# Layer 0 attention: q's rms norm moved from the projected q to the exponential's factor

## The chip, the cores and the metric

The kernel runs on one core of one Trainium2 chip. Five engines of that core work side by side and wait for each other by semaphores: TensorE (PE; its weight loads are listed apart, as PEld), VectorE (DVE), ScalarE (ACT), GpSimd (POOL) and SyncE (SP), which starts most transfers. The metric is the time of one execution on the device in microseconds (us). Three executions of the kernel before took 2746.94, 2752.83 and 2753.98 us; their median is 2752.83 us.

## The reference

The program is a trunk of four layers on 512 latent tokens and 256 context tokens of width 1024, each layer with another mixer (attention, neighbourhood attention, convolution, Fourier) and an MLP. The change is in the mixer of layer 0 alone. Cut to what matters there:

```python
def rms_norm(x, g):
    y = xf * lax.rsqrt(jnp.mean(xf * xf, axis=-1, keepdims=True) + EPS)
    return (y * g.astype(jnp.float32)).astype(x.dtype)

def gqa_attend(q, k, v):
    s = jnp.einsum('bqkgd,bnkd->bkgqn', q, k, preferred_element_type=jnp.float32)
    p = jax.nn.softmax(s, axis=-1).astype(v.dtype)
    return jnp.einsum('bkgqn,bnkd->bqkgd', p, v)

def gqa_mixer(hl, hc, ang, w_qkv, q_g, k_g, w_o, ctx_out):
    scale = HEAD_DIM ** -0.5
    ql = apply_rope(rms_norm(ql.reshape(B, S, AT_HEADS, HEAD_DIM), q_g), ang) * scale
    kl = apply_rope(rms_norm(kl.reshape(B, S, AT_KV_HEADS, HEAD_DIM), k_g), ang)
    ...
    qc = rms_norm((hc @ w_qkv[:, :AT_WIDTH]).reshape(B, C, AT_HEADS, HEAD_DIM), q_g) * scale
    oc = gqa_attend(qc.reshape(B, C, AT_KV_HEADS, AT_GROUP, HEAD_DIM), kc, vc)
```

There are 16 query heads of 64 columns. The norm divides each query's 64 values by one number, which is a factor common to all scores of that query and head.

## The kernel before

Matrix products are made in two parts each (a value rounded to fp32r and its remainder), so that one product costs three matmuls (`mm3`, lines 119 to 127: L124, L125, L127).

**Projection stage (`l0a`).** Keys and values are already in PSUM when it begins. Then come the queries in 12 units: four groups of columns `g` by three pairs of token tiles `tp` (`tp` 0 and 1 are the latent tokens, `tp` 2 the context). A unit is 48 matmuls into one PSUM bank (`ps_mm`, four banks in turn, so that the matmuls of a unit can start when the bank of the unit four before it has been read for the last time). Units are collected in `wait`; after every second one `finish` handles both. `qk_norm` squares a unit on ScalarE (L490) and sums by head on VectorE (L491), for both units, and calls `rstd` once: a square root on ScalarE (L133) and five small VectorE instructions (L135 to L139). `qk_unit` then multiplies the PSUM bank by the result on VectorE (L499), which is the last read of the bank, and rotates: for `tp` below 2 two GpSimd products (L511), a VectorE product (L512) and a GpSimd sum (L513); for `tp` 2 only a VectorE product with the gain (L515). ScalarE rounds the unit (L104 of `split`, into `pk`), VectorE takes the remainder (L105), TensorE transposes (L527), ScalarE copies out (L529), and a DMA stores it to HBM (L530). Beside this VectorE works off products for the modulation vectors (L223).

**Attention stage (`l0b`).** It takes over the four banks of `ps_mm` as two buffers `ps_s` of two banks each. The work is 8 pairs of heads; a pair is 12 fronts (128 queries of one head): 8 fronts with 768 keys and 4 of the context with 256 keys. A front is: score matmuls (L612), the negated maximum on VectorE (L614, `small_m`), the exponential on ScalarE with that maximum as bias and with the row sum as a second output (L616), TensorE transposes of the result `p` (L621), and for each group of up to three transposes a rounding copy on ScalarE (L104) and a remainder on VectorE (L105), both into `pt`. The products with v follow one head later (L635), and a closing per head pair (L555, L557, L559, L561, L567, L568, L573).

**What sets the order.** The program is not run in the order in which it is written: a scheduler reorders the instructions of each engine when the kernel is built, from its own estimate of durations; only instructions marked to keep their order (the loads among them) stay. Every engine then works its list strictly in order, so an instruction that waits holds up all behind it on that engine. The last two query units are finished inside the attention's loop (`late`, at `i == LATE`).

## Time and profile before

| | |
|---|---|
| median of three executions | 2752.83 us |
| the profiled execution's own time | 2748.76 us |
| its span | 2747.0 us |
[...]
| busy share TensorE, VectorE, ScalarE, GpSimd | 96%, 65%, 42%, 15% |
| projection of q, taken as 79 to 183 us | 104.0 us |
| attention, taken as 183 to 384.4 us | 201.4 us |

A row of the timeline gives start, length, engine, line, operation and tiles (output<-inputs), and in brackets the idle time before it with what ended it. TensorE's matmuls overlap in the pipeline: a row's length (0.28 us for 256 columns) is more than the distance from one start to the next (0.12 us). On VectorE and ScalarE too the next instruction may start a little (0.08 to 0.1 us) before the end of the one before. The profiled execution is one of the kernel's, and 4.07 us below the median of the three.

### The profile page before, as it was taken

How to read it: one execution, taken by the hardware profiler on the slowest of the kernel's cores; microseconds unless marked ns; L12 is line 12 of the kernel's file. 1: busy time of each engine (PE TensorE's matmuls, PEld its weight loads, DVE VectorE, ACT ScalarE, POOL GpSimd, SP SyncE). 2: the span in 40 equal slices, each digit the busy share in tenths (PEclk: the TensorE clock that was granted, in tenths of full speed). 3: DMA queues.
4: the chain of work that ended last, by engine and by line, in shares of the span. 5: the costliest groups of instructions: out<-in, count | busy, mean ns of one | idle time of the engine just before them, and what ended most of it. 6: DMA issues, size and time to landing. Idle time of an engine off the chain costs nothing.

```text
span 2747.0 us, 39895 instructions
## 1 busy us (share of the span) xinstructions
PE 2638.0 (96%) x15472; PEld 2316.5 (84%) x15472; DVE 1776.1 (65%) x2827; ACT 1154.8 (42%) x2052; POOL 405.4 (15%) x359
## 2 busy tenths in 40 slices
PE   7989899999999999998999999998999998999998
PEld 5878778888888888988988889888888887988888
DVE  7988879766453372268766657998666657644445
ACT  3458864212121342268523335656322245533323
POOL 2321212000000030034200004543000012200002
PEclk8999999999999999999999999999999999999999
DMA  7431234445442256488466644213466633333334
GB/s 269 133 123 36 77 120 147 139 145 153 137 140 85 77 168 209 138 201 190 161 206 207 190 147 139 77 47 107 133 212 200 206 124 107 123 115 94 98 100 123
DMA packets 124844, 384.85 MB, mean 140 GB/s; under 512 B 17264, under 2 KB 37872, under 8 KB 123632
## 3 DMA queue, kind: packets, MB, share of 16 engines
q1 hardware_dynamic: 121392, 379.17, 44.2%
q10 hardware_dynamic: 3264, 3.15, 0.3%
q8 instruction: 122, 2.00, 0.3%
q14 instruction: 66, 0.54, 0.1%
HBM read 354.98 MB, written 27.26 MB: 139 GB/s over the span
## 4 chain that ended last, share of the span: by engine, by line
PE 49%; DVE 4%; DMA 2%; ACT 1%; issue 0%; POOL 0%; DVEq 0%; SPq 0%; ACTq 0%; POOLq 0%
PE ps_mm L124 15%; PE ps_mm L125 15%; PE ps_mm L127 15%; DVE ps_st L1162 1%; DMA k<-k 1%; DMA q<-q 1%; PE ps_cv L124 1%; PE ps_cv L125 1%; PE ps_cv L127 1%; DVE h L182 0%; PE ps_s L881 0%; PE ps_pt L890 0%; PE ps_cv L995 0%; PE ps_cv L998 0%; PE ps_cv L999 0%
## 5 line engine op out<-in xcount | busy, mean ns | idle before, releaser
L104 ACT CAST wh<-raw 128x1024 fp32r<-128x1024 f32 (+1 forms) x397 | 419.6, 1060 | 1030.6 <-PE ps_mm L125 606.5
L105 DVE TENSOR_TENSOR wl<-raw,wh 128x1024 fp32r<-128x1024 f32 (+1 forms) x368 | 463.7, 1262 | 372.6 <-ACT wh L104 369.5
L194 POOL TENSOR_TENSOR S<-S,tmp_q 128x256 f32<-128x256 f32 (+1 forms) x104 | 144.8, 1392 | 1684.8 <-ACT tmp_q L193 1680.7
L124 PE MATMUL ps_mm<-u,wh 128*128 128x512 f32 (+1 forms) x1088 | 374.9, 346 | 0.0
L125 PE MATMUL ps_mm<-u,wh 128*128 128x512 f32 (+1 forms) x1088 | 373.8, 345 | 0.0
L127 PE MATMUL ps_mm<-u,wl 128*128 128x512 f32 (+1 forms) x1088 | 373.6, 346 | 0.0
L125 PE MATMUL ps_mm<-hm,wh 128*128 128x512 f32 (+1 forms) x912 | 331.2, 365 | 0.0
L127 PE MATMUL ps_mm<-hm,wl 128*128 128x512 f32 (+1 forms) x912 | 331.0, 365 | 0.0
L124 PE MATMUL ps_mm<-hm,wh 128*128 128x512 f32 (+1 forms) x912 | 328.2, 366 | 1.1 <-ACT hm L181 1.1
L223 DVE CUSTOM_DVE_ANT_0 prod<-araw,sb 128x1024 bf16<-128x1024 f32 x224 | 276.4, 1234 | 6.5 <-DMA araw<-in_ada 5.3
L206 DVE SCALAR_TENSOR_TENSOR x<-ps_mm,mod,x 128x256 f32<-128x256 f32 (+1 forms) x192 | 115.1, 605 | 246.8 <-PE ps_mm L127 241.1
L125 PEld LDWEIGHTS ps_mm<-u,wh 128*128 128x128 f32 x1088 | 206.1, 189 | 25.0
L127 PEld LDWEIGHTS ps_mm<-u,wl 128*128 128x128 f32 x1088 | 205.9, 189 | 25.2
L124 PEld LDWEIGHTS ps_mm<-u,wh 128*128 128x128 f32 x1088 | 205.7, 189 | 25.3 <-DVE x L206 0.4
L127 PEld LDWEIGHTS ps_mm<-hm,wl 128*128 128x128 f32 x912 | 172.6, 189 | 27.6 <-DVE wl L105 0.4
L125 PEld LDWEIGHTS ps_mm<-hm,wh 128*128 128x128 f32 x912 | 172.7, 190 | 27.2
L124 PEld LDWEIGHTS ps_mm<-hm,wh 128*128 128x128 f32 x912 | 170.8, 190 | 28.7 <-ACT hm L181 1.5
L104 ACT CAST u<-tmp_r 128x512 fp32r<-128x512 f32 (+2 forms) x143 | 89.0, 624 | 171.1 <-DVE tmp_r L738 170.9
L124 PE MATMUL ps_big<-hm,wh 128*128 128x512 f32 x464 | 157.4, 339 | 0.8 <-ACT wh L104 0.8
L105 DVE TENSOR_TENSOR u<-tmp_r,u 128x512 fp32r<-128x512 f32 (+2 forms) x143 | 99.1, 695 | 86.6 <-ACT u L104 86.2
L125 PE MATMUL ps_big<-hm,wh 128*128 128x512 f32 x464 | 145.9, 337 | 0.0
L124 PE MATMUL ps_mm<-wh,h 128*128 128x256 f32 x448 | 129.9, 291 | 7.3 <-DVE tmp_r L499 2.9
(311 smaller groups left out, 5781.6 us busy)
## 6 DMA issues: line engine op xcount, KB each, us to landing
raw<-in_w SPq DMA_DIRECT2D x288, 512.0 KB, 3.9
araw<-in_ada SPq DMA_DIRECT2D x176, 512.0 KB, 3.7
raw<-in_wo SPq DMA_DIRECT2D x32, 512.0 KB, 4.3
raw<-in_wpw SPq DMA_DIRECT2D x24, 512.0 KB, 3.5
raw<-in_wqk SPq DMA_DIRECT2D x16, 512.0 KB, 4.1
q<-q SPq DMA_DIRECT2D x32, 256.0 KB, 9.1
raw<-in_wft SPq DMA_DIRECT2D x16, 512.0 KB, 3.8
k<-k SPq DMA_DIRECT2D x32, 224.0 KB, 9.4
```

Source lines behind the costliest of these rows:

```text
L104: self.nc.scalar.copy(out=H, in_=src)
L105: (low or self.nc.vector).tensor_tensor(out=L, in0=src, in1=H.bitcast(F), op=ALU.subtract)
L124: mm(o, lhs[0], rh, start=(k == 0), stop=False)
L125: mm(o, lhs[0], rl, start=False, stop=False)
L127: mm(o, lhs[1], rh, start=False, stop=last)
L194: (add or nc.gpsimd).tensor_tensor(out=S[:, :w], in0=S[:, :w], in1=q, op=ALU.add)
L206: self.nc.vector.scalar_tensor_tensor(out=xm, in0=self.like(ps), scalar=gate[:, m:m + 1], in1=xm, op0=ALU.mult, op1=ALU.add)
L223: ins = self.nc.vector.tensor_tensor_reduce(out=junk, in0=t, in1=self.sb[:, v], op0=ALU.mult, op1=ALU.add, scale=1.0, scalar=0.0, accum_ou ...
L1162: keep(nc.vector.scalar_tensor_tensor(out=y if last else a, in0=ut, scalar=wt, in1=a, op0=ALU.mult, op1=ALU.add))
```

## The change

The sum of squares and `rstd` remain, but q's result no longer multiplies q. It is kept by query and head in a new tile `rsq` (four groups of 24 numbers), and the attention uses it twice per front: a new VectorE instruction (L630) multiplies the negated maximum by it, and the exponential (now L632) takes it as its factor. In `qk_unit` the multiplication of q (12 of the 15 at L499; it stays for k, now L505) is gone. For `tp` below 2 ScalarE copies the bank to SBUF (L509), GpSimd's two products (L523) read that copy, and VectorE's own product (now L525) reads the bank itself; for `tp` 2 the product with the gain (now L528) reads the bank. `rstd` is called once per group of three units (four times, on 24 columns) where it was called once per two (six times, on 16). Units are finished one by one and not in twos; only the last two wait for `late`.

```diff
         ve.tensor_tensor(out=v, in0=v, in1=y, op=ALU.mult)
         ve.tensor_tensor(out=v, in0=v, in1=y, op=ALU.mult)
-        last = ve.scalar_tensor_tensor(out=y, in0=v, scalar=1.5, in1=y, op0=ALU.add, op1=ALU.mult)
+        out = y if out is None else out
+        last = ve.scalar_tensor_tensor(out=out, in0=v, scalar=1.5, in1=y, op0=ALU.add, op1=ALU.mult)
         if pin:
             self.tc.keep_in_program_order(last)
-        return y
+        return out
 
     def bcast(self, cols, nb):
...
@@ -446,15 +448,23 @@
         for tp in range(3):
             pv = self.kv_ps[1][tp].rearrange("p (t h d) -> p t h d", t=2, h=4)
             self.split(pv, *(self.vp[:, 2 * tp:2 * tp + 2, :, s] for s in range(2)))
-        rs = self.qk_norm(self.kv_ps[0])
+        ss = self.small(24, "h")
         for tp in range(3):
-            self.qk_unit(self.kv_ps[0][tp], rs[tp], tp, 1, 0, wk, tab, qkg)
+            self.squares(self.kv_ps[0][tp], ss, tp)
+        rs = self.rstd(ss, HD, "h")
+        for tp in range(3):
+            self.qk_unit(self.kv_ps[0][tp], rs[:, 8 * tp:8 * tp + 8], tp, 1, 0, wk, tab, qkg)
             self.pump(1)
-        wait = []
+        wait, sums = [], {}
 
         def finish():
-            for a, r in zip(wait, self.qk_norm([a[0] for a in wait])):
-                self.qk_unit(a[0], r, a[1], 0, a[2], wk, tab, qkg)
+            for ps, tp, g in wait:
+                if tp == 0:
+                    sums[g] = self.small(24, "h")
+                self.squares(ps, sums[g], tp)
+                self.qk_unit(ps, None, tp, 0, g, wk, tab, qkg)
+                if tp == 2:
+                    self.rstd(sums[g], HD, "h", out=self.rsq[:, g])
                 self.pump(1)
             wait.clear()
 
@@ -468,7 +478,7 @@
                     for k in range(KC):
                         self.mm3([o], (h[k][:, 0, t0:t0 + P], h[k][:, 1, t0:t0 + P]), [(W[0][:, k], W[1][:, k])], k, k == KC - 1)
                 wait.append((ps, tp, g))
-                if len(wait) == 2 and (g, tp) != (3, 2):
+                if g < 3 or tp == 0:
                     finish()
         self.drain()
 
...
@@ -480,24 +490,26 @@
         self.close("h0", "ada", "wide")
         self.open_weights(3)
 
-    def qk_norm(self, pss):
+    def squares(self, ps, ss, tp):
+
+        sq = self.tmp("q")
+        self.nc.scalar.activation(sq, ps, AF.Square)
+        self.nc.vector.tensor_reduce(out=ss[:, 8 * tp:8 * tp + 8], in_=sq.rearrange("p (n d) -> p n d", d=HD), axis=AX.X, op=ALU.add)
+
+    def qk_unit(self, ps, rs, tp, a, g, wk, tab, qkg):
+
 
         nc = self.nc
-        n = len(pss)
-        ss = self.small(8 * n, "h")
-        for i, ps in enumerate(pss):
-            sq = self.tmp("q")
-            nc.scalar.activation(sq, ps, AF.Square)
-            nc.vector.tensor_reduce(out=ss[:, 8 * i:8 * i + 8], in_=sq.rearrange("p (n d) -> p n d", d=HD), axis=AX.X, op=ALU.add)
-        rs = self.rstd(ss, HD, "h")
-        return [rs[:, 8 * i:8 * i + 8] for i in range(n)]
-
-    def qk_unit(self, ps, rs, tp, a, g, wk, tab, qkg):
-
-        nc = self.nc
-        qn = self.tmp("r")
-        nc.vector.tensor_tensor(out=qn.rearrange("p (n d) -> p n d", d=HD), in0=ps.rearrange("p (n d) -> p n d", d=HD),
-                                in1=rs.unsqueeze(2).to_broadcast([P, 8, HD]), op=ALU.mult)
+        if rs is not None:
+            qn = self.tmp("r")
+            nc.vector.tensor_tensor(out=qn.rearrange("p (n d) -> p n d", d=HD), in0=ps.rearrange("p (n d) -> p n d", d=HD),
+                                    in1=rs.unsqueeze(2).to_broadcast([P, 8, HD]), op=ALU.mult)
+        elif tp < 2:
+            qn = self.tmp("r")
+            nc.scalar.copy(out=qn[:, :512], in_=ps)
+        else:
+            qn = ps
+        qn = qn[:, :512]
         q4 = qn.rearrange("p (t h d) -> p t h d", t=2, h=4)
         o = self.newS()
         o4 = o.rearrange("p (t h d) -> p t h d", t=2, h=4)
@@ -509,7 +521,8 @@
                 q5 = q4[:, t].rearrange("p h (s e) -> p h s e", s=2)
                 s5 = tab[:, a, 1, c].rearrange("p (s e) -> p s e", s=2).unsqueeze(1).to_broadcast([P, 4, 2, HD // 2])
                 nc.gpsimd.tensor_tensor(out=b4[:, t].rearrange("p h (s e) -> p h s e", s=2), in0=q5[:, :, ::-1, :], in1=s5, op=ALU.mult)
-            nc.vector.tensor_tensor(out=o4, in0=q4, in1=tab[:, a, 0, 2 * tp:2 * tp + 2].unsqueeze(2).to_broadcast([P, 2, 4, HD]), op=ALU.mult)
+            c4 = q4 if rs is not None else ps.rearrange("p (t h d) -> p t h d", t=2, h=4)
+            nc.vector.tensor_tensor(out=o4, in0=c4, in1=tab[:, a, 0, 2 * tp:2 * tp + 2].unsqueeze(2).to_broadcast([P, 2, 4, HD]), op=ALU.mult)
             nc.gpsimd.tensor_tensor(out=o, in0=o, in1=b, op=ALU.add)
         else:
             nc.vector.tensor_tensor(out=o.rearrange("p (n d) -> p n d", d=HD), in0=qn.rearrange("p (n d) -> p n d", d=HD),
@@ -612,8 +625,11 @@
                     nc.tensor.matmul(ps[:, c0:c1], q[:, hh, t0:t0 + P], self.kd[:, pair // 2, s, c0:c1], start=(s == 0), stop=(s == 1))
             mx = self.small(1, "m")
             nc.vector.tensor_reduce(out=mx, in_=ps[:, kc:TALL], axis=AX.X, op=ALU.max, negate=True)
+            n = part * 8 + u * 4 + pair % 2 * 2 + hh
+            rs = self.rsq[:, pair // 2, n:n + 1]
+            nc.vector.tensor_tensor(out=mx, in0=mx, in1=rs, op=ALU.mult)
             p = wk.tile([P, TALL], F, tag="p", name="p", bufs=3)
-            nc.scalar.activation(p[:, kc:], ps[:, kc:TALL], AF.Exp, bias=mx, accum_out=sums[:, u, hh:hh + 1])
+            nc.scalar.activation(p[:, kc:], ps[:, kc:TALL], AF.Exp, bias=mx, scale=rs, accum_out=sums[:, u, hh:hh + 1])
             for c in range(k0, 6, 3):
                 n = min(3, 6 - c)
                 pp = self.ps("st")

```

The build order shows three places. The first is VectorE at the end of the projection stage, from the sums of squares of the last unit to the first maximum of the attention. Before:

```order
L491 TENSOR_REDUCE small_h<-tmp_q 128x8
L135 TENSOR_SCALAR small_hv<-small_h 128x16
L136 RECIPROCAL small_hy<-small_hr 128x16
L137 TENSOR_TENSOR small_hv<-small_hv,small_hy 128x16
L138 TENSOR_TENSOR small_hv<-small_hv,small_hy 128x16
L139 SCALAR_TENSOR_TENSOR small_hy<-small_hv,small_hy 128x16
L499 TENSOR_TENSOR tmp_r<-ps_mm,small_hy 128x512 x2
L512 TENSOR_TENSOR S<-tmp_r,tab 128x512
L515 TENSOR_TENSOR S<-tmp_r,qkg 128x512
L614 TENSOR_REDUCE small_m<-ps_s 128x1 x2
```

In the changed kernel, from the last but one unit's product on (the squares are now L497, the maximum L627):

```order
L525 TENSOR_TENSOR S<-ps_mm,tab 128x512
L105 TENSOR_TENSOR pk<-S,pk 128x8x64
L497 TENSOR_REDUCE small_h<-tmp_q 128x8
L528 TENSOR_TENSOR S<-ps_mm,qkg 128x512
L135 TENSOR_SCALAR small_hv<-small_h 128x24
L136 RECIPROCAL small_hy<-small_hr 128x24
L137 TENSOR_TENSOR small_hv<-small_hv,small_hy 128x24
L138 TENSOR_TENSOR small_hv<-small_hv,small_hy 128x24
L105 TENSOR_TENSOR pk<-S,pk 128x8x64
L140 SCALAR_TENSOR_TENSOR rsq<-small_hv,small_hy 128x24
L627 TENSOR_REDUCE small_m<-ps_s 128x1
L630 TENSOR_TENSOR small_m<-small_m,rsq 128x1
```

Before, the last reads of the PSUM banks (L499) stand behind the five small instructions; now the last reads (L525 and L528) stand ahead of them, and the small instructions have only the first maximum behind them.

The second is VectorE inside the attention, from maximum 27 to maximum 29 of 96 (the third pair of heads). Before:

```order
L614 TENSOR_REDUCE small_m<-ps_s 128x1
L105 TENSOR_TENSOR pt_2696<-ps_st,pt_2695 128x384 x2
L568 TENSOR_TENSOR tmp_t<-ps_pv,tmp_t 64x256
L614 TENSOR_REDUCE small_m<-ps_s 128x1
L105 TENSOR_TENSOR pt_2696<-ps_st,pt_2695 128x384 x2
L614 TENSOR_REDUCE small_m<-ps_s 128x1
L568 TENSOR_TENSOR tmp_t<-ps_pv,tmp_t 64x256
```

In the changed kernel:

```order
L627 TENSOR_REDUCE small_m<-ps_s 128x1
L105 TENSOR_TENSOR pt_2693<-ps_st,pt_2692 128x384
L630 TENSOR_TENSOR small_m<-small_m,rsq 128x1
L581 TENSOR_TENSOR tmp_t<-ps_pv,tmp_t 64x256
L105 TENSOR_TENSOR pt_2693<-ps_st,pt_2692 128x384 x2
L627 TENSOR_REDUCE small_m<-ps_s 128x1
L630 TENSOR_TENSOR small_m<-small_m,rsq 128x1
L105 TENSOR_TENSOR pt_2760<-ps_st,pt_2759 128x384
L627 TENSOR_REDUCE small_m<-ps_s 128x1
L568 RECIPROCAL rs<-sums 128x4
L630 TENSOR_TENSOR small_m<-small_m,rsq 128x1
```

The new product L630 stands behind its maximum L627, in most fronts not straight behind it but with one or more others between them (a remainder L105 here, the reciprocal of a head pair there).

The third is ScalarE at the same place, exponentials 27 to 29. The number in `pt` names the head: 2695 is that of exponentials 25 and 26; 2760 before and 2759 after that of exponentials 27 and 28. Before:

```order
L616 ACTIVATE p,sums<-ps_s,small_m 128x768
L104 CAST pt_2695<-ps_st 128x384 x2
L567 COPY tmp_t<-ps_pv 64x256
L561 COPY tmp_r<-ps_st 128x256
L616 ACTIVATE p,sums<-ps_s,small_m 128x768
L104 CAST pt_2760<-ps_st 128x384 x2
L616 ACTIVATE p,sums<-ps_s,small_m 128x768
```

In the changed kernel:

```order
L632 ACTIVATE p,sums<-ps_s,small_m,rsq 128x768
L574 COPY tmp_r<-ps_st 128x256
L104 CAST pt_2759<-ps_st 128x384
L104 CAST o_1_1921<-tmp_t 128x256
L632 ACTIVATE p,sums<-ps_s,small_m,rsq 128x768
L104 CAST pt_2759<-ps_st 128x384 x2
L632 ACTIVATE p,sums<-ps_s,small_m,rsq 128x768
```

Before, the copies between exponential 27 and 28 were those of exponential 26's front, and the copies of front 27 came behind exponential 28. Now a copy of front 27 itself (the first `pt_2759`) stands between exponentials 27 and 28, and one of front 28 between 28 and 29: most long exponentials now have a copy of the front just ahead of them on ScalarE's list before them.

## Rows read from the trace of the kernel before

**Rows 1.** busy us by engine: start:end length, PE, PEld, DVE, ACT, POOL, clock, DMA

```profile
79.00:183.00 104.00, 91.56 (x712) 89.13 (x712) 97.12 (x161) 44.69 (x74) 37.74 (x30) 0.94 0.45 148
183.00:384.40 201.40, 179.86 (x1274) 159.17 (x1274) 174.03 (x354) 174.00 (x454) 39.18 (x48) 0.97 0.13 45
236.36:260.04 23.68, 21.84 (x159) 19.34 (x159) 21.41 (x45) 21.05 (x57) 4.43 (x6) 1.00 0.10 35
```

**Rows 2.** TensorE's waits in 78:183: who waited, for whom, us in total, times, longest

```profile
PE ps_s L612 <- DVE tmp_r L499: 4.3, 1, 4.3
...
PE ps_mm L124 <- DVE tmp_r L499: 2.9, 2, 1.8
...
PE ps_st L527 <- DVE pk L105: 1.0, 1, 1.0
```

**Rows 3.** timeline, TensorE: start us, us, engine line op [idle before <-releaser]

```profile
145.96 0.39 PE L124 MATMUL ps_mm<-wh,h 128*128 128x256 f32 x1 [1.75 <-DVE tmp_r L499]
```

**Rows 4.** the windows around that stop, columns as in rows 1

```profile
147.40:150.90 3.50, 3.50 (x19) 3.50 (x18) 3.26 (x8) 1.18 (x3) 1.59 (x2) 0.51 1.00 386
150.90:168.00 17.10, 17.00 (x146) 16.80 (x145) 17.02 (x28) 6.72 (x12) 8.11 (x6) 1.00 0.53 182
```

**Rows 5.** instructions grouped by line in 78:183: busy us, mean ns of one

```profile
L104 ACT CAST pk<-S 128x512 fp32r<-128x512 f32 x10 | 6.1, 620 | 11.6 <-POOL S L513 10.2 <-DVE S L515 1.4
...
L499 DVE TENSOR_TENSOR tmp_r<-ps_mm,small_hy 128x512 f32<-128x512 f32 x14 | 9.0, 685 | 0.3
```

**Rows 6.** timeline, VectorE, end of the projection stage

```profile
171.97 0.68 DVE L105 TENSOR_TENSOR pk<-S,pk 128x512 fp32r<-128x512 f32 x1
...
176.66 0.69 DVE L491 TENSOR_REDUCE small_h<-tmp_q 128x8 f32<-128x512 f32 x1 [1.50 <-ACT tmp_q L490]
...
180.03 1.29 DVE L499 TENSOR_TENSOR tmp_r<-ps_mm,small_hy 128x512 f32<-128x512 f32 x2
```

**Rows 7.** timeline, ScalarE, the same stretch

```profile
176.03 0.60 ACT L490 ACTIVATE tmp_q<-ps_mm 128x512 f32<-128x512 f32 x1 [0.62 <-PE ps_mm L127]
...
178.71 0.31 ACT L133 ACTIVATE small_hr<-small_h,eps 128x16 f32<-128x16 f32 x1
179.03 1.28 ACT L616 ACT_TABLE_LOAD   x1
184.13 0.90 ACT L616 ACTIVATE p<-ps_s,small_m 128x768 f32<-128x768 f32 x1 [3.82 <-DVE small_m L614]
```

**Rows 8.** instructions grouped by line in five attention periods: busy us, mean ns

```profile
L105 DVE TENSOR_TENSOR pt<-ps_st,pt 128x384 fp32r<-128x384 f32 x80 | 42.7, 549 | 3.3 <-ACT pt L104 2.4
...
L614 DVE TENSOR_REDUCE small_m<-ps_s 128x1 f32<-128x768 f32 x41 | 38.9, 949 | 0.3
...
L104 ACT CAST pt<-ps_st 128x384 fp32r<-128x384 f32 x80 | 37.4, 489 | 6.0 <-PE ps_st L621 5.7
...
L616 ACT ACTIVATE p<-ps_s,small_m 128x768 f32<-128x768 f32 x40 | 36.5, 913 | 0.1
...
L616 ACT ACTIVATE p<-ps_s,small_m 128x256 f32<-128x256 f32 x20 | 9.8, 491 | 0.4
```

**Rows 9.** timeline, ScalarE, one exponential in the attention

```profile
235.31 0.91 ACT L616 ACTIVATE p<-ps_s,small_m 128x768 f32<-128x768 f32 x1
```

**Rows 10.** timeline, TensorE, the transposes behind it, and one pair later

```profile
236.36 0.55 PE L621 MATMUL ps_st<-ident,p 128*128 128x128 f32 x3 [0.40 <-ACT p L616]
...
260.04 0.55 PE L621 MATMUL ps_st<-ident,p 128*128 128x128 f32 x3 [0.39 <-ACT p L616]
```

**Rows 11.** timeline, VectorE: small instructions, unchained and chained

```profile
122.04 0.16 DVE L135 TENSOR_SCALAR small_hv<-small_h 128x16 f32<-128x16 f32 x1
122.12 0.24 DVE L136 RECIPROCAL small_hy<-small_hr 128x16 f32<-128x16 f32 x1
...
149.93 0.18 DVE L137 TENSOR_TENSOR small_hv<-small_hv,small_hy 128x16 f32<-128x16 f32 x1
150.14 0.17 DVE L138 TENSOR_TENSOR small_hv<-small_hv,small_hy 128x16 f32<-128x16 f32 x1
```

More of the change, by code (lines that the diff above doesn't have):

```diff
@@ L127, in mm3, with rstd @@
             mm(o, lhs[1], rh, start=False, stop=last)
-    def rstd(self, ss, n, role="n", pin=False):
+    def rstd(self, ss, n, role="n", pin=False, out=None):
         w = ss.shape[-1]
@@ L433, in l0a @@
         self.vp = kv.tile([P, 6, 4, 2, HD], R, name="vp")
+        self.rsq = kv.tile([P, 4, 24], F, name="rsq")
         self.qd = self.dram.tile([8, P, 2, TALL], F, name="qd")
```

## The prediction

> **What bounds the kernel now.** I read the table of the page first: TensorE is busy 96% of the span, so outside the two stages of the change there is little to win, and the change's effect has to be looked for in the busy times by stretch [rows 1]. In the projection stage (79 to 183 us) VectorE is busy 97.12 of 104.00 us and TensorE 91.56; ScalarE has more than half of its time free. So TensorE sets the pace there, with VectorE close behind it: TensorE's list of waits says on whom it stops [rows 2]. It stopped 4.3 us once, at the handover to the attention, and 2.9 us in two stops, both for L499, the multiplication of q that the change takes out, and 1.0 us for a remainder (`pk`). The reader is to see that it is not L499's own length that costs: 0.685 us [rows 5]. The instruction is late because the sums of two units, a square root and five small instructions have to come first.
>
> In the attention everything is balanced: in one head pair's period VectorE is busy 21.41 of 23.68 us, ScalarE 21.05, TensorE 21.84 [rows 1]. TensorE restarts at the same point of the pattern at 236.36 and 260.04, each time after a stop for an exponential [rows 10], which is where I take the period of 23.68 from. No engine is full, so the period is set by the three waiting for each other; anything that is added to the path from the scores to the exponential can lengthen it.
>
> **Part 1, the two stops of the projection stage.** A bank is now free once ScalarE has squared and copied it and VectorE has made one product of it, within its own unit, and it is wanted again only four units later. The two stops go: 2.9 us [rows 2]. [...]
>
> **Part 2, the handover.** Before: the last unit is squared at 176.03 [rows 7], its sum starts at 176.66 [rows 6], the square root only gets its turn at 178.71 behind copies [rows 7], L499 reads the banks at 180.03 [rows 6], and the first exponential starts at 184.13 [rows 7]. After, from the same 176.03: sum to 177.35 (176.66 + 0.69); the product out of PSUM, not shown before but of L499's form, 0.685 [rows 5], to 178.0; the rounding copy 0.62 [rows 5], to 178.65; the remainder 0.68 [rows 6], to 179.35; the last small instruction 0.18 [rows 11], to 179.5; the maximum 0.95 [rows 8], to 180.45; the new product 0.2, to 180.65, and then the exponential. The load of the exponential's table, 1.28 us [rows 7], fits between the copy and that. 184.13 - 180.65 = 3.5 us gained. What is late next is no longer the norm of q but this chain of remainder and maximum.
>
> **Part 3, what the projection stage gets in exchange.** Eight copies on ScalarE, not shown before; the nearest row is the square of the same form, 0.60 us [rows 7], 4.8 us in all. ScalarE has 59 us free there [rows 1], which hides them; uncovered, all on TensorE's path, they would cost 4.8. VectorE loses 12 x 0.685 = 8.2 us and two of six chains of small instructions; that is cover, not path. Nearer to zero, because a bank has four units of time: I take 0.7 us for a new wait behind a copy. Bounds: 0 and 4.8.
>
> The sum of parts 1 to 3: -2.9 - 1.3 - 3.5 + 0.7 = -7.0 us, between -7.7 and -2.9.
>
> **Part 4, the attention.** There are 96 new VectorE products on one column. No row shows that shape. The nearest are the small instructions of 16 columns: 0.08 us from one start to the next if they don't depend on each other (122.04 to 122.12), 0.21 if they do (149.93 to 150.14) [rows 11]. Twelve per pair are 1.0 to 2.5 us of VectorE, which has 23.68 - 21.41 = 2.3 us idle. In the build order only 15 of the 96 stand straight behind their maximum, so most cost 0.08 of VectorE's time; but a remainder in between (0.549, [rows 8]) delays the exponential by about as much more. The product also waits for that remainder's copy.
>
> The second thing is ScalarE's new order. From an exponential to its transposes it is 1.05 us (235.31 [rows 9] to 236.36 [rows 10]), 0.55 more until three transposes are done [rows 10], and a copy holds ScalarE about 0.39 (0.489 less the overlap of 0.1, [rows 8]). Where the next exponential stands behind one copy of its own predecessor's front it can start 2.0 us after that, behind two 2.4. In a pair's eight long fronts I count three behind two (7.2), three behind one (6.0), one behind one and another copy (2.4) and one behind none (1.3): 16.9 us. For the four short ones, with an exponential of 0.49 in place of 0.91 [rows 8], I estimate 1.4 each by the same chain: 5.6. Together 22.5 against a period of 23.68; two or three fronts per pair in which the new product also waits for a remainder fill the rest, so the new chain nearly fills the period without passing it. Bounds for a period: -1.2 (the chain alone sets it) and +2.5 (each product chained and on the path). I take +0.5, nearer to the lower end, because VectorE's idle time covers the cheap products and the chain is still under the period. Eight pairs: +4 us, between -10 and +20.
>
> [...]
>
> **Sum.** -7.0 + 4 = -3.0 us on the profiled execution's 2748.76: 2745.8. That execution lies 4.07 us below the median of its kernel, so in medians it is 2750 us.
>
> **The rivals.** (1) *The exponential's path sets the period and each new product lies on it*, slower: 12 x 0.21 = 2.5 us per pair, 20 in all, less 7.0: +13, 2766 us. For it: TensorE's stops in the period are for exponentials [rows 10], all three engines are near full [rows 1], and the chain above leaves little of the period. Against it: most products aren't chained, and VectorE has 2.3 us. It decides from a period of about 25.6 us on, since 15 us in eight pairs outweigh the 7 by more than 8. (2) *The attention hides it all, or even follows the shorter chain*, faster: -7.7, and -0.5 per pair, some half of the lower bound, is -4: -11.7, 2741 us. For it: the sum of the chain, 22.5. Against: any queueing adds to a chain of three nearly full engines. (3) *The banks aren't freed earlier*: ScalarE's list is in order, and a copy that waits there for GpSimd or behind the next unit's square holds the bank as L499 did. Then parts 1 and 3 give nothing, and -3.5 + 4 is about 0: 2753 us. For it: ScalarE's small gaps are where the list waits, as with the square root that came at 178.71 [rows 7]; against it: four units of slack.
>
> **How the numbers follow.** Forecast 0.50, rival 1 0.17, rival 2 0.23, rival 3 0.10. The forecast's own range is 2744 to 2757: the gain of the projection between -7.7 and -4, the attention between 0 and +8. The range that should hold eight times in ten reaches to rival 2 and short of rival 1: 2740 to 2763. What a measurement of this kernel can tell from no change is about 0.3%, 8.3 us: faster means below 2744.6, slower above 2761.1. Faster: most of rival 2 and a little of the forecast, 0.23. Slower: rival 1, 0.17. The rest, 0.60, is within.
>
> **What would show it.** Parts 1 and 2: in the changed profile TensorE has no stops of over 1 us for a read of a `ps_mm` bank, no stretch at half clock near 147, and the first exponential starts at about 177 (184.1, less 7.7 to 7.0). Part 3: no wait of TensorE for the copies L509. Part 4: the distance between equal points of two pairs is 23.2 to 24.7 us; the new product is 0.16 to 0.18 long. A period of 25.6 or more makes rival 1 right, one of 23.4 or less rival 2; a first exponential at 180 or later makes rival 3 right. A change of the time outside 79 to 385 us would be one that I have no step for.

## The result and the profile after

The kernel after takes 2783.14 us in the median of 4 runs (2781.09 to 2788.41), the one before 2749.89 us beside it: ratio 1.0124, 95% interval 1.0101 to 1.0147. The change made the kernel slower by 33 us, where 2750 us was predicted, in a range of 2740 to 2763. The profiled execution of after took 2788.41 us with a span of 2786.6, 39.6 us over that of before (2747.0); it is the slowest of the four, 5.3 us above their median. The profiled execution of the run called e18 was disturbed, so that of e18 only the times of its other executions are used.

Where the 39.6 us lie is read from the start of every twelfth exponential, the first of each head pair. The last entry runs to the end of the last exponential.

```
             first    length of pair 1 to 8, us
before      184.13    27.54 23.64 23.68 23.64 23.65 23.65 27.97 22.32
after       181.75    30.96 30.44 26.97 27.12 27.15 27.14 33.90 32.28
```

The attention starts 2.4 us earlier and its eight pairs take 39.9 us longer. Behind it the two differ by 2.1 us (2366.8 and 2368.9). So the loss is in the attention, 3.5 us in a steady pair and more in the first two and the last two.

Busy times of after, the projection stage and three steady pairs, and the same three pairs of before; columns as in [rows 1]:

```profile
79.00:181.75 102.75, 89.31 (x712) 86.96 (x712) 89.05 (x145) 49.05 (x82) 36.21 (x30) 0.97 0.45 150
...
270.12:351.53 81.41, 67.86 (x477) 59.07 (x475) 71.82 (x169) 68.20 (x168) 13.33 (x18) 1.00 0.09 31
```

```profile
258.99:329.93 70.94, 65.36 (x476) 57.94 (x476) 64.16 (x133) 63.15 (x169) 13.29 (x18) 1.00 0.11 35
```

No engine is nearer to full than before: VectorE 88% in place of 90, TensorE 83 in place of 92. The engines wait for each other more. Who waits in those three pairs of after (engine and line, for whom: us in total, times, longest), and TensorE's wait for the exponential in the same three pairs of before:

```profile
PE ps_st L637 <- ACT p L632: 10.9, 15, 1.4
```

```profile
ACT p L632 <- DVE small_m L630: 6.6, 15, 0.7
ACT pt L104 <- PE ps_st L637: 5.7, 12, 0.6
```

```profile
PE ps_st L621 <- ACT p L616: 2.2, 6, 0.4
```

TensorE's wait for the exponential was 2.2 us before and is 10.9 after; ScalarE's wait for the product did not exist. Instructions of those pairs, grouped by line and form (busy us, mean ns), answering to [rows 8]:

```profile
L632 ACT ACTIVATE p<-ps_s,small_m,rsq 128x768 f32<-128x768 f32 x24 | 24.0, 999 | 2.9 <-DVE small_m L630 2.8
...
L630 DVE TENSOR_TENSOR small_m<-small_m,rsq 128x1 f32<-128x1 f32 x36 | 10.0, 278 | 0.3
...
L632 ACT ACTIVATE p<-ps_s,small_m,rsq 128x256 f32<-128x256 f32 x12 | 6.8, 566 | 3.8 <-DVE small_m L630 3.8
```

The exponential with a factor per query takes 999 and 566 ns where it took 913 and 491. The product takes 278 ns in the mean, 10.0 us in three pairs.

The handover, ScalarE and VectorE of after, answering to [rows 6, 7]:

```profile
175.88 0.60 ACT L496 ACTIVATE tmp_q<-ps_mm 128x512 f32<-128x512 f32 x1 [2.01 <-PE ps_mm L127]
...
177.88 0.62 ACT L104 CAST pk<-S 128x512 fp32r<-128x512 f32 x1 [0.34 <-DVE small_hv L135]
180.46 1.28 ACT L632 ACT_TABLE_LOAD   x1 [1.96 <-DVE small_m L630]
181.75 0.99 ACT L632 ACTIVATE p<-ps_s,small_m,rsq 128x768 f32<-128x768 f32 x1
```

```profile
178.53 0.69 DVE L105 TENSOR_TENSOR pk<-S,pk 128x512 fp32r<-128x512 f32 x1
...
179.24 0.95 DVE L627 TENSOR_REDUCE small_m<-ps_s 128x1 f32<-128x768 f32 x1
180.22 0.16 DVE L630 TENSOR_TENSOR small_m<-small_m,rsq 128x1 f32<-128x1 f32 x1
```

The last unit is squared 0.15 us earlier than before (176.03), so the projection stage itself gained next to nothing; the handover gained 2.2 us. Its chain ends with the product at 180.4. Then the table load, which before ran at 179.03 while others worked, waits for the product and only then takes its 1.28 us.

TensorE's waits in 78:183, answering to [rows 2]:

```profile
PE ps_st L637 <- ACT p L632: 4.0, 1, 4.0
PE ps_st L560 <- DVE pk L553: 2.7, 2, 2.2
...
PE ps_st L540 <- DVE pk L105: 1.5, 1, 1.5
PE ps_s L625 <- DVE small_hv L135: 1.4, 1, 1.4
PE ps_st L540 <- ACT qs L542: 1.2, 2, 0.7
```

No wait for L499 is left, and none for a copy L509. One wait of the scores (L625) at the handover is put down to L135, the first of the norm's small instructions; it stands straight behind L528, the last unit's last read of its bank, and ends 0.1 us after it. In place of the stops for L499 TensorE waits for remainders of k and q (`pk`). The 2.2 us stop that ends at 112.88 shows why: on VectorE's list the remainders L553 stand behind a weight remainder of 2.28 us and, ahead of that, a product for the modulation vectors of 1.21 us (107.88). TensorE and VectorE of after:

```profile
112.88 1.52 PE L560 MATMUL ps_st<-ident,pk 128*128 128x128 f32 x8 [2.18 <-DVE pk L553]
```

```profile
109.02 2.28 DVE L105 TENSOR_TENSOR wl<-raw,wh 128x2048 fp32r<-128x2048 f32 x1
...
111.52 1.22 DVE L553 TENSOR_TENSOR pk<-S,pk 128x512 fp32r<-128x512 f32 x2
```

Behind that stop TensorE's granted clock falls to half, as it did behind the L499 stop in [rows 4], where after now shows full clock (columns as in [rows 1]):

```profile
113.34:116.70 3.36, 3.13 (x15) 2.73 (x14) 3.36 (x6) 1.68 (x4) 1.88 (x2) 0.50 0.00 0
147.40:150.90 3.50, 3.00 (x26) 2.80 (x25) 3.50 (x7) 1.79 (x4) 2.22 (x1) 1.00 1.00 387
```

### The profile page after: what moved, and what is told of

It reads as the page before. It is cut to its first block, busy times and chain, and to the rows that moved or that the text cites. A ratio compares the mean times of both kernels' runs of the same rounds, so it can differ in the third digit from the quotient of the medians.

```text
span 2786.6 us, 40017 instructions
## 1 busy us (share of the span) xinstructions
PE 2652.6 (95%) x15472; PEld 2326.6 (83%) x15472; DVE 1783.4 (64%) x2901; ACT 1172.6 (42%) x2058; POOL 402.9 (14%) x359
## 4 chain that ended last, share of the span: by engine, by line
PE 79%; DVE 10%; DMA 4%; ACT 4%; issue 2%; POOL 0%; SPq 0%; DVEq 0%; ACTq 0%; POOLq 0%
PE ps_mm L124 18%; PE ps_mm L125 18%; PE ps_mm L127 18%; PE ps_big L124 6%; PE ps_big L127 6%; PE ps_big L125 6%; DVE prod L224 2%; DVE small_m L627 1%; DMA k<-k 1%; DVE pt L105 1%; ACT p L632 1%; PE ps_pv L651 1%; PE ps_st L637 1%; DVE h L183 1%; PE ps_cv L124 1%
## 5 line engine op out<-in xcount | busy, mean ns | idle before, releaser
L105 DVE TENSOR_TENSOR wl<-raw,wh 128x1024 fp32r<-128x1024 f32 (+1 forms) x368 | 462.9, 1260 | 375.7 <-ACT wh L104 372.9
L127 PEld LDWEIGHTS ps_mm<-hm,wl 128*128 128x128 f32 x912 | 172.6, 190 | 27.6 <-DVE wl L105 0.4
L105 DVE TENSOR_TENSOR u<-tmp_r,u 128x512 fp32r<-128x512 f32 (+2 forms) x143 | 99.0, 695 | 86.5 <-ACT u L104 86.2
```

Source lines behind the costliest of these rows:

```text
L105: (low or self.nc.vector).tensor_tensor(out=L, in0=src, in1=H.bitcast(F), op=ALU.subtract)
L127: mm(o, lhs[1], rh, start=False, stop=last)
```

## The experiments

Theory A: the product made the build put the instructions in another order, and the order makes the period. Theory B: the product's and the longer exponential's own time makes it. Theory C: the projection leaves something behind. All ratios are to the kernel before, with their 95% interval; a period is that of a steady pair, 23.65 us before and 27.13 after.

**Which part of the change.** e1 is the kernel after less L630 and less `scale=rs`; e2 is the kernel before with `rsq` filled with ones and these lines of after, e6 and e7 the same with one of the two:

```diff
+            nc.vector.tensor_tensor(out=mx, in0=mx, in1=rs, op=ALU.mult)
-            nc.scalar.activation(..., bias=mx, accum_out=...)
+            nc.scalar.activation(..., bias=mx, scale=rs, accum_out=...)
```

> The kernel after without the product of the maximum and without the exponential's factor: the projection and the handover as changed, the attention's instructions as before. It leaves q's norm out of the scores. Theory A (the added product made the builder order ScalarE's list otherwise: a front's own copies now stand ahead of the next exponential, and the chain exponential, transposes, copy, exponential sets the period) and theory B (the product's and the longer exponential's own time sets it) expect the same here: first exponential at about 181.8 us, a pair's period of 23.65 us as before, the whole 2.4 us under the kernel before, 2747 us. Theory C (the changed projection leaves something behind that slows the attention, as other places of its tiles or a later load): period above 25 us, over 2765 us.

Measured (e1): 2745.73 us, 0.9985 (0.9975 to 0.9996); first exponential 181.02, period 23.65; C falls. The kernel gains 1 to 7 us by the interval, but the profiled execution does not show that all of it is the projection's: the first exponential comes 3.1 us earlier and the attention ends only 0.7 us earlier (379.5 in place of 380.2). Its first pair is longer, at a lower granted clock; first pair of before and of e1:

```profile
184.13:211.67 27.54, 23.39 (x160) 21.02 (x161) 20.95 (x41) 21.80 (x54) 1.69 (x3) 0.92 0.20 66
```

```profile
181.02:210.73 29.71, 25.60 (x160) 23.68 (x161) 20.21 (x39) 21.20 (x52) 1.46 (x2) 0.83 0.18 63
```

In before and after alike TensorE, which had stood still at the handover (4.3 us [rows 2] and 4.0), has a granted clock of 0.50 from 182 to 188 and of 1.00 from 189 on, though the first exponential starts at 184.13 and at 181.75. The first pair of e1 has 0.83 in the mean where that of before has 0.92, so that the earlier first exponential gives part of its lead back.

> The kernel before, with the attention alone changed: a factor tile of ones, the product of each maximum with it, and the exponential with it as its factor. Theories A and B: the whole loss without the projection's gain: first exponential at 184.1 us, period 27.1 us, attention 35 to 38 us longer, 2785 to 2790 us. Theory C: period under 25 us and under 2765 us.

Measured (e2): 2785.09 us, 1.0125 (1.0108 to 1.0142); period 27.13, first exponential 185.80, 1.7 us later than expected. The whole loss is in these two lines.

> The kernel before with the 96 products (by ones) and no factor in the exponential. Here too the build order puts own copies ahead of the next exponential, in 36 of 60 steady fronts (in the kernel after 48 of 60; in the kernel before none). Theory A: most of the loss stays, period 25.5 to 27 us, 2768 to 2785 us; exponential 0.91 us again. Theory B with the longer exponential as the main cost: period 24.7 us at most (12 products at 0.08 to 0.15 us), 2760 us at most.

Measured (e6): 2789.74 us, 1.0140 (1.0124 to 1.0155); the five middle pairs take 27.6 to 35.1 us, uneven, so worse than A's own figure, though fewer exponentials stand behind own copies than in the kernel after. What makes them uneven was not looked into.

> The kernel before with the exponential's factor (a tile of ones) and no product. The build order has no own copy ahead of the next exponential, as before. Theory A: period 23.65 us plus 1.0 us at most (12 exponentials 0.085 us longer each), 2750 to 2758 us. Theory B with the longer exponential as the main cost: period 26 us or more, 2770 us or more. The exponential of 768 columns takes 1.00 us in place of 0.91 by both.

Measured (e7): 2755.91 us, 1.0021 (1.0012 to 1.0030); period 23.77, exponentials of 1008 and 579 ns. The factor costs 0.09 us an exponential and 0.1 us a pair. In its profiled execution the eight pairs together take 2.5 us longer (198.6 in place of 196.1); the rest of the 6 us lies outside the attention, and no cause for it was looked for. It is the product that costs.

**Order or time.** The build can be given edges that only fix the order on one engine, without a wait. e11 chains the kernel before (no product) into the order of after; e12 chains the kernel after, product included, into that of before:

```diff
+        for text in (ORDER_DVE, ORDER_ACT, ORDER_PE):
+            last = None
+            for label in text.split():
+                for ins in self.names[label]:
+                    if last is not None:
+                        self.tc.add_manual_dep(ins, last.name, <order only>)
+                    last = ins
```

> The kernel before (no product, no factor), whose attention instructions are chained, without any new wait, into the order that the build gave the kernel after: TensorE's scores and transposes, VectorE's maxima, remainders and tail, ScalarE's exponentials, copies and tail. Theory A (the order that the build chose because of the product makes the period, not the product's own time): period 26 to 27 us, 2770 to 2785 us. Theory B (the product's own time, its stretching beside GpSimd and its place on VectorE's list make it): period 23.6 to 24.4 us, 2750 to 2756 us.

Measured (e11): 2775.99 us, 1.0098 (1.0078 to 1.0117); period 27.8. The order alone, without a product, costs 4.1 us a pair. Not all of that is waiting: the granted clock of three steady pairs is 0.94 in the mean, where those of the kernel after have 1.00. The first steady pair of e11, up to a stretch at half clock and in it (columns as in [rows 1]):

```profile
268.67:275.00 6.33, 4.44 (x32) 3.86 (x31) 5.07 (x11) 4.61 (x13) 1.48 (x2) 0.99 0.01 2
275.00:278.50 3.50, 3.50 (x16) 3.21 (x15) 1.94 (x4) 1.85 (x6) 0.73 (x1) 0.52 0.02 5
```

TensorE had been busy 4.44 of 6.33 us before its clock fell. The rest of this pair has 115 matmuls in 17.87 us, 0.155 us each; at that rate 22.5 would have fitted into the stretch in place of 16, which makes it cost 1.0 us. By the two pairs of e26 shown below it costs 1.6. Both are estimates. At full clock the order alone would then cost 2.5 to 3.1 us a pair.

> The kernel after with everything that it changed, product and factor too, but its attention instructions chained into the order of the kernel before, each product straight behind its maximum. Theory A: period 23.8 us (the 0.1 that the longer exponential alone has shown) to 24.8 us (some of the product), first exponential at 181 to 182 us, 2748 to 2757 us. Theory B: period 25.5 us or more, 2765 us or more.

Measured (e12): 2762.31 us, 1.0052 (1.0032 to 1.0071); period 25.2, first exponential 183.57. The same instructions as after, in the old order, cost 1.5 us a pair, 0.1 of it the factor. That is a little over what A allowed and under what B did. The two costs don't add up (4.1 + 1.5 for 3.5). Part of the excess is e11's half clock, which the kernel after doesn't have; for the rest the new order leaves VectorE idle time that can take the product in, which is argued and not shown. Three steady pairs of e11 and of e12, columns as in [rows 1]:

```profile
268.67:351.99 83.32, 70.26 (x476) 62.88 (x475) 66.36 (x133) 64.22 (x170) 13.33 (x18) 0.94 0.09 31
```

```profile
263.85:339.28 75.43, 65.75 (x476) 58.22 (x475) 70.56 (x169) 66.85 (x170) 13.30 (x18) 1.00 0.10 35
```

VectorE is busy 80% of e11's pairs and 94% of e12's.

**The stretched products.** e5 writes the product as `nc.vector.tensor_scalar(out=mx, in0=mx, scalar1=rs, ...)`; e18 is e12 with that line.

> The kernel after with the product written as a tensor times a scalar per partition (one operand in memory and one scalar) in place of two tensors; the build order is nearly the same (21 products straight behind their maximum in place of 15). Theory D (the products that lasted 0.70 to 0.75 us beside GpSimd's work, in place of 0.15, set the period): the long ones go, period 25.5 us or less, 2770 us or less. Theory A: period 26.7 to 27.2 us, 2780 to 2787 us, whether the long ones go or not.

Measured (e5): 2767.52 us, 1.0065 (1.0050 to 1.0080); period 26.9, the last pairs 30.8 and 25.7. All 96 products, of after and of e5 (min, median, max ns):

```profile
L630 DVE TENSOR_TENSOR small_m<-small_m,rsq x96: 140/150/745, 180.2 to 416.9; 128x1 f32<-128x1 f32 x96
```

```profile
L630 DVE TENSOR_SCALAR small_m<-small_m,rsq x96: 182/204/215, 180.6 to 404.7; 128x1 f32<-128x1 f32 x96
```

The stretching is gone, the steady period stays. D falls for the period; for the whole its mark (2770 us or less) was met and A's missed, some 15 us better than after, most of it in the second pair and the last two. I had not expected that, and as the build order is not quite the same, it does not show whether the stretching or the order is what these pairs gained by.

> The kernel after in the order of before, as in the earlier run with 25.2 us, but with the product as a tensor times a scalar per partition (0.20 us each, none stretched beside GpSimd) in place of two tensors (0.16 us, eleven of them 0.3 to 1.9). Theory A2 (VectorE's time is what the product costs in this order): 12 x 0.20 = 2.4 us of VectorE per pair in place of 2.65, so 24.9 to 25.2 us, 2755 to 2762 us. Theory D (the stretched products are the cost): under 24.3 us, under 2755 us.

Measured (e18): 1.0065 (1.0045 to 1.0086), 2761.67 to 2774.04 us. Not faster than e12, so D falls in the old order too. Whether the period is A2's, no trace shows.

> The kernel after in the order of before, with the product on GpSimd in place of VectorE. VectorE is relieved of 2.4 us per pair; the path from the maximum to the exponential gets two hand-overs between engines in place of one, and GpSimd's tail (4.4 us per pair) may stand ahead of a product. Theory A2 (VectorE's time): period 23.8 to 24.6 us, under 2756 us. Theory E (the length of the path from maximum to exponential): period 25.5 us or more, 2765 us or more.

Measured (e17): 2759.72 us, 1.0033 (1.0023 to 1.0042); period 24.8. VectorE is relieved (busy 64.58 of 74.40 us in three pairs, 70.56 of 75.43 in e12), and of the 1.4 us that e12 lies above the 23.77 of the factor alone, 1.0 stay: above A2's figure and below E's. Time on VectorE can't be the whole cost; how much of it the way over GpSimd stands for (a product takes 190 ns there in the median, 159 on VectorE in e12) was not separated.

**Which list.** Here the lists of the kernel after are chained one or two at a time in the kernel before (e19 to e22, e26), and those of the kernel before one at a time in the kernel after (e24, e25).

> The kernel before with only ScalarE's exponentials and copies chained into the order of the kernel after; TensorE's and VectorE's lists are left to the build. Theory A (the exponential behind copies of its predecessor's own front makes the period): 27 us or more, as in the run with all three lists chained (27.7), 2770 to 2785 us. Theory F (VectorE's or TensorE's list is what costs): 25 us or less, 2760 us or less.

Measured (e19): 2759.75 us, 1.0036 (1.0023 to 1.0048); period 24.56. ScalarE's list alone costs 0.9 us: A in this form falls.

> The kernel before with only VectorE's maxima, remainders and tail chained into the order of the kernel after (the product left out); TensorE's and ScalarE's lists left to the build. Theory G (VectorE's list: the remainders of a front stand ahead of the maximum of the next but one, so a maximum waits for copies): 26.5 us or more per pair. Theory H (TensorE's list: the scores of a front stand behind all transposes of the front two before it, so behind that front's exponential; here in 24 of 60 steady fronts, in the kernel after in 49, in the kernel before in none): 24 to 25.5 us.

Measured (e20): 2779.81 us, 1.0109 (1.0089 to 1.0129); period 27.6, at full clock, the size that G says. But VectorE's waits in three pairs of it are most of all those of the folds (L598) for ScalarE's copy, and only then those of the remainders (L128):

```profile
DVE tmp_t L598 <- ACT tmp_t L597: 10.2, 9, 1.6
DVE pt L128 <- ACT pt L127: 4.1, 9, 0.9
DVE small_m L646 <- PE ps_s L644: 1.2, 3, 0.4
```

> The kernel before with only TensorE's scores and transposes chained into the order of the kernel after (49 of 60 scores behind all transposes of the front two before). Theory H: 26.5 us or more per pair. Theory G: 24 to 25 us, as in the run that chained ScalarE's exponentials and copies alone (24.56, where the build put 46 of 60 scores so by itself; that already speaks against H unless the value matmuls' places matter too).

Measured (e21): 2760.65 us, 1.0042 (1.0024 to 1.0060); period 25.6, between the two theories.

> The kernel before with TensorE's and ScalarE's lists chained into the order of the kernel after and VectorE's left to the build, which comes to the same list but for the places of the reciprocals, their spreading and one remainder per six fronts. Theories G and H: 27 us or more, as with all three chained (27.7). Theory J (only the place of VectorE's tail, the sums' reciprocals and folds, matters): 25 us or less.

Measured (e22): 2773.39 us, 1.0091 (1.0071 to 1.0111); steady period 24.9, but 35.0 and 29.9 us in the last two pairs. Moving a few places on VectorE's list (the tail and a remainder) takes 2.9 us off a steady pair of e11, as J says; with them the half clock of those pairs went (1.00 in the mean of four pairs), which is 1.0 to 1.6 of it by the estimates above. The last pairs keep the loss.

> The kernel before with only VectorE's maxima and remainders chained into the order of the kernel after, its tail (reciprocals, spreadings, folds) left to the build, which places several folds behind the maximum that they stood ahead of. Theory K (it is the folds, which wait for ScalarE's copy and with it hold up the maxima behind them): 25.5 us or less. Theory L (it is the remainders ahead of the maxima): 26.5 us or more.

Measured (e26): 2767.45 us, 1.0068 (1.0048 to 1.0088); periods 26.2 to 27.9. Two of its pairs that follow each other, at full clock and with a stretch at half clock, and VectorE's longest wait in three pairs:

```profile
266.91:293.15 26.24, 21.81 (x158) 19.41 (x158) 21.36 (x45) 21.78 (x56) 4.41 (x6) 1.00 0.09 32
293.15:320.97 27.82, 23.36 (x158) 20.87 (x158) 21.65 (x45) 21.77 (x56) 4.39 (x6) 0.94 0.09 28
```

```profile
DVE pt L124 <- ACT pt L123: 9.4, 15, 1.0
```

At full clock the period lies between the marks of K and L. The maxima and remainders alone still cost some 2.6 us a pair there, and the remainders do wait for ScalarE's copies: K falls, and so it is not the folds alone.

> The kernel after, product and factor included, with only TensorE's scores and transposes chained into the order of the kernel before; the build then leaves 48 of 60 steady exponentials without an own copy ahead (in the kernel after 12) and 24 of 96 products straight behind their maximum. Theory H: most of the order's cost goes, 25 to 25.8 us per pair, 2755 to 2768 us. Theory G: 26.5 us or more, 2775 us or more.

Measured (e24): 2777.10 us, 1.0108 (1.0088 to 1.0128); pairs of 25.0 and 26.4 us at full clock, and of 27.5 and 27.6 with a mean of 0.94. The time is G's, the pairs at full clock are not. TensorE's old list alone does not mend the kernel.

> The kernel after, product and factor included, with only VectorE's list chained into the order of the kernel before (each product straight behind its maximum); TensorE's and ScalarE's lists are left to the build. Theory G (VectorE's list is what the order costs): 24.8 to 25.5 us per pair, as with all three lists in the old order (25.2), 2755 to 2766 us. If TensorE's and ScalarE's lists matter as much: 26 us or more, 2770 us or more.

Measured (e25): 2776.84 us, 1.0104 (1.0084 to 1.0124); period 26.9, as said for the case that the other lists matter as much. Nor does VectorE's list mend it. G falls as a cause by itself: VectorE's list out of the new order is enough to lose, and TensorE's or VectorE's out of the old, alone, is not enough to win. Which pair of lists would do was not tried.

**Versions without the product.** e13 multiplies the norm on q behind the rope. e15 keeps the change, but lets one instruction do maximum and product:

```diff
-            nc.vector.tensor_reduce(out=mx, in_=ps[:, kc:TALL], axis=AX.X, op=ALU.max, negate=True)
-            nc.vector.tensor_tensor(out=mx, in0=mx, in1=rs, op=ALU.mult)
+            nc.vector.tensor_scalar(out=ps[:, kc:TALL], in0=ps[:, kc:TALL], scalar1=rs, scalar2=None,
+                                    op0=ALU.mult, op1=ALU.min, accum_out=mx)
```

with `rs` negated once per group and `scale=-1.0` in the exponential.

> Another place for the norm: q goes from PSUM straight into the rope as in the kernel after, and the norm is multiplied on q behind the rope, in SBUF, with the sum, square root and small instructions of each unit beside the rope; the attention is that of the kernel before. Theories A and B: the attention keeps the period of 23.65 us, and the projection keeps most of what the change gained there (the bank no longer waits for the norm), less what VectorE does more (12 products and 6 more chains of small instructions, some 0.685 + 0.6 us each): first exponential at 181 to 186 us, 2745 to 2752 us. Theory C (VectorE's list is what the projection waits for): first exponential at 187 us or later, 2755 us or more.

Measured (e13): 2751.92 us, 1.0004 (0.9994 to 1.0014); period 23.65, first exponential 185.74. As expected, and no gain.

> The kernel after without the extra instruction: one VectorE instruction multiplies the scores in their bank by minus the factor per query and keeps the minimum, which is the exponential's bias; the exponential has the constant factor -1. The build order has 56 of 60 steady exponentials without an own copy ahead of them, nearly as before. Theory A2 (of the 3.5 us per pair the order is the larger part, and with the order of before what the product takes from VectorE's 2.3 idle us is the smaller one): both parts go, period 23.6 to 24.2 us if this instruction is as long as the maximum was (0.95 us), first exponential at 181 to 183 us, 2744 to 2752 us. If writing the bank makes it longer, its excess counts eight times a pair: at 1.15 us VectorE would be busy 23 us of a pair, period 24.5 to 25 us, 2755 to 2760 us. Theory E (the attention follows a path from scores to exponential that any longer norm of q lengthens): 25 us or more.

Measured (e15): 2751.60 us, 1.0010 (1.0000 to 1.0020); period 23.9, first exponential 183.05. The build gave it nearly the old order, and the loss is gone. Four pairs of it, grouped by line:

```profile
L629 DVE TENSOR_SCALAR_CACHE_REDUCE ps_s<-ps_s,rsq 128x768 f32<-128x768 f32 x32 | 32.6, 1018 | 1.6 <-PE ps_s L625 1.3
...
L629 DVE DVE_READ_ACCUMULATOR ps_s<-ps_s,rsq 128x1 f32 x48 | 6.7, 139 | 0.0
```

The instruction is 0.07 us longer than the maximum was and brings a second of 0.14 that reads its minimum out; VectorE's 0.9 us more per pair cost 0.2. It beats the kernel after, and the kernel before is level with it or up to 0.2% faster. No version that keeps the norm beat the kernel before.

## Why the prediction was wrong

The failed step is part 4, "+0.5 us" a pair: it is +3.5 in the steady pairs and +39.9 in all eight, beyond even the bound of +20. Its terms, one by one:

- *ScalarE's new order.* "Together 22.5 against a period of 23.68 ... the new chain nearly fills the period without passing it." With ScalarE's new list alone (e19) the period is 24.56, 2 us over that sum; whether the chain itself is longer or the other lists' waits come on top was not separated. Worse, it was the only list whose cost was worked out. All three lists of the new order together give 27.8 without a product, 26.2 to 26.8 by estimate without the half clock that comes with it. VectorE's list had been read in the build order, but only for the product's place on it.
- *The product.* Its length was right, 150 ns in the median against 0.16 to 0.18; 21 of 96 were longer than 0.3, which no row of before could show. In the old order it costs 1.4 us a pair with its place on the path, within the bounds (-1.2 to +2.5) and above the value taken.
- *The exponential's factor* had no price at all: 0.09 us each, 0.1 us a pair.
- *The first and last pairs* were given the price of steady ones. They lost 3.4, 6.8, 5.9 and 10.0 us, 26 of the 39.9. In e11, without a product, the last two lost 7.7 and 5.3; the order is the larger part there too. The last pair has its granted clock at 0.89 in place of 1.00, a part of its loss that the prediction did not think of.

Parts 1 to 3, "-7.0", came out at -2.4 at the first exponential, and e1 shows that part of such a lead is lost again in the first pair, at a mean clock of 0.83; the prediction had no term for that. In part 1 the two stops for L499 and the half clock near 147 went as said, but the stage ended only 0.15 us earlier: waits for remainders grew from 1.0 us to 4.2, and behind one of them the clock was 0.50 for 3.36 us. The 1.3 us that the sum has for the half clock near 147 are an estimate from [rows 4] (19 matmuls in 3.50 us, where 30 fit at the rate of the 17.10 us behind); no run shows the term by itself. After has 26 matmuls in those 3.50 us, at a clock of 1.00, and 15 in the 3.36 us at 0.50. The stops were counted as time at the stage's end without asking what VectorE's new list delays. In part 2 the chain was right to 0.3 us (the product ends at 180.4, forecast 180.65); "the load of the exponential's table ... fits between" was wrong, it waits for the product and adds 1.28. In e1, without product and factor, the load runs at 179.32 and the handover from last square to exponential is 4.34 us (before 8.10, after 5.87). With the factor and no product (e7), or with the product on GpSimd (e17), it does not wait either, so it is not the factor that it waits for. In after, e5 and e12 the product on VectorE held up, beside the exponentials, one instruction at their line that has no tile, for 2.0 us; in after it is the load. In e2 and e6, which have that product too, there is no such wait. What makes the load take part in it stays open. The load in e1, e7 and e17:

```profile
179.32 1.28 ACT L631 ACT_TABLE_LOAD   x1
```

```profile
179.75 1.28 ACT L620 ACT_TABLE_LOAD   x1
```

```profile
179.18 1.28 ACT L688 ACT_TABLE_LOAD   x1
```

Part 3, no wait for the copies, was right.

Of the rivals, the first is the nearest: by its own mark, a period over 25.6, it decides, but its 2766 us is still 17 short. Its mechanism, each product on the path, is nearest to e12, the product in the old order (2762 us), and is the smaller part. The third's mark (first exponential after 180) was met, but not by banks that stay busy: the stage ended only 0.15 us earlier, with new waits for remainders, and even without the table load the exponential could not have started before 180.4, when the product ended. What the prediction had no rival for is that an order costs without the instruction that brought it. What stays open is which waits within the new order are the needed ones, since the lists cost 0.9, 2.0 and 3.9 us alone and 4.1 together (2.5 to 3.1 by estimate at full clock). No run chained a kernel into its own order; that the edges cost nothing by themselves is therefore assumed, and the 1.5 us of e12 may hold some of it.

## What to carry to other kernels

Where three engines are each some 90% busy and pass work around, the order in which a build lists their work can be worth more than the instruction that changed it, as here: compare the order on every engine, and if it moved, pin the old one and measure that first. An instruction between producer and consumer is worth folding into the one ahead of it: here that left the order nearly alone too (the fused minimum took the ratio from 1.0124 to 1.0010). Price the edges of a stage, its first and last rounds, apart from its steady part. Before two periods are compared, look at the granted clock of each.

## What the runs showed of the hardware

An operand per partition in place of a constant made the exponential longer by nearly the same amount at both widths: 95 ns on 768 columns (913 in before [rows 8], 1008 in e7) and 88 on 256 (491 and 579).

A one-column product of two tensors in SBUF, 0.15 us long, lasted up to 0.745 where GpSimd worked in SBUF at the same time; each of the 21 of after that were longer than 0.3 ran beside a GpSimd instruction. VectorE and GpSimd of after:

```profile
296.44 0.71 DVE L630 TENSOR_TENSOR small_m<-small_m,rsq 128x1 f32<-128x1 f32 x1
```

```profile
296.39 0.74 POOL L586 TENSOR_TENSOR tmp_t<-tmp_t,tmp_r 128x256 f32<-128x256 f32 x1 [6.36 <-DVE tmp_t L581]
```

Both end together, at 297.1. With one tensor and a scalar per partition (e5) none of the 96 passed 0.215 us.
